# Feed-forward of a hybrid retention and attention layer: steps placed by product number, and other buffer counts

## Chip, cores and metric

The kernel runs on one core of one Trainium2 chip. Time is device microseconds of one execution. The kernel before was run three times: 3031.91, 3032.76 and 3039.37 us, median 3032.76. A separate execution was profiled; all rows of the profile are of that one.

## The reference, cut to what matters

One layer over 2048 positions of width 1024, with 256 positions of context. After a norm and a modulation, one projection gives the inputs of a retention in both directions (4 heads) and of an attention over context and sequence (8 heads). Their outputs go through `w_out` and are added to x. Then comes the part that the change rewrites:

```python
h2 = _modulate(_rmsnorm(x, norm2_g), sh2, sc2)
x = x + g2 * _sqrelu_mlp(h2, w_ff1, w_ff2)      # square(relu(h @ w1)) @ w2, 4096 wide
return _rmsnorm(x, final_norm_g)
```

## The kernel before

**Stages.** The first 690 us make the projections. From there to 1644 us the attention runs in numbered steps, with the retention and the output projection placed between its steps. The feed-forward fills the rest: *up products* (`h @ w1`) to 2358, then *down products* (`@ w2`) to 3008.

**Arithmetic.** Each f32 operand is split in an f16 `hi` and an f16 remainder `lo` (ACT copies `hi`, another engine subtracts it to get `lo`), and three f16 matmuls (hi·hi, hi·lo, lo·hi) stand for one. On top of that, blocks of 2 by 2 are multiplied with seven products in place of eight: sums of the operands' blocks are formed first, and sums of the seven products give the four results. So a *product* here is 4 x 3 = 12 matmuls of 128 x 512 in one PSUM bank, and each weight or activation block has four sums and seven *forms* (a form is a `hi` and `lo` pair).

**Up.** The 2048 positions are two halves (`hs[0]`, `hs[1]`) whose seven h forms lie in SBUF. w1 is taken in 16 blocks of 256 columns. `ITEMS` lists the work: the first `AHEAD` = 6 blocks for half 0 alone, ten blocks for both halves, and the first six again for half 1, since half 1's h forms are made later. 22 items, 32 block-halves, 224 products. For each item, `fetch_w1` (L1470) loads two tiles of w1, `sum_w1` (L1477, POOL) makes four sums, `form_w1` makes seven forms (L1487 ACT, L1488 DVE), and `up_part` (L1503 to L1505) does the matmuls. `up_out` takes a product out of PSUM: product 0 by an ACT copy (L1525), the others by DVE adds (L1515). A finished block gets its relu (L1519, ACT) and square (L1520, POOL) and is stored in DRAM as `u` (L1544).

Two more jobs run beside this: `h_pair(1, j)` makes half 1's h forms (L1368 POOL sums, L70 and L71 forms), and `w2_steps` makes the forms of w2 (L1554 loads, L1559 POOL sums, L1563 and L1564 forms, L1570 stores to `wf`).

**Down.** Four rounds `rd`, each with four of the 16 w2 blocks, and in each eight pairs of position tiles: 32 pairs, 224 products. `fetch_w2` (L1670) loads a round's seven 1 MB weight forms, `fetch_u` (L1680) a pair's four `ur` blocks, `fetch_y` (L1690) its two rows of x. `prepare(p, i)` makes the sums (L1694 POOL) and the form i of pair p (L70, L71). `down` (L1715 to L1717) does the matmuls, `down_out` takes them out (L1733 ACT copy for product 0, L1728 DVE adds), and `gate` multiplies by g2 and adds to y (L1755, L1756, both POOL, but the last ones DVE). y is stored after each round. In round 3 the final norm follows: ACT squares (L1764), a DVE sum (L1776), two small POOL operations for the root (L1009, L1010), a DVE scaling (L1782), the store (L1785).

**Order.** Each engine works through its own queue in program order, and the program order is written by hand (`manual_schedule`). Attention steps are placed in a table by step number and phase (`on`, `run`). The feed-forward is not: `up_jobs` and `down_jobs` are loops that emit, for each product, its matmuls, then the next item's sum and form, then `up_out` or `down_out`, and then a few steps from lists (`rest`, `pairs`, `later`, `gates`, `written`). All of a form, or all of a gate with its square, is emitted in one go. SP issues nearly all DMAs, also in program order.

A buffer *ring* hands out slots of several pools in turn: `w` for forms (7, with 3 more late), `r` for results (6, with 5 more), PSUM banks (4, with 2 more). Pools of the side `xp` have tags with a count each: `xr` 3, `hb` 2, `hp` 2, `w1s` 4, `hu` 3, `u` 2.

Of the kernel before, what the change touches and what calls it, by code (L numbers as in the profile page):

```python
# [22 lines left out]
P = 128  # L23
# [17 lines left out]
POOL_PAIRS = (0, 2, 4, 6, 7)  # L41

# [12 lines left out]
def layer_kernel(ctx: ExitStack, tc: tile.TileContext, a: dict, out: bass.AP):  # L55
# [1154 lines left out]
    def output_weights(k0):  # L1210
# [3 lines left out]
        def gates(i):  # L1214
            g = w_["g", i] = xp.tile([P, D], F32, name="g1b", tag="hb", bufs=2)
            nc.sync.dma_start(g, g1_d[i].partition_broadcast(P))

        def fetch(k, n):
            w = xp.tile([P, 2, 512], F32, name="wos", tag="xr", bufs=3)
            src = a["w_out"][0, k * P : (k + 2) * P, n * 512 : (n + 1) * 512]  # L1220
            nc.sync.dma_start(w, src.rearrange("(k p) n -> p k n", p=P))
            w_[k, n], w_[k + 1, n] = w[:, 0], w[:, 1]
# [25 lines left out]
    def output_tile(t, k, last):  # L1248
        y = {}

        def fetch_x():
            y["x"] = xp.tile([P, D], F32, name="xr", tag="xr", bufs=3)
            nc.sync.dma_start(y["x"], a["x"][0, t * P : (t + 1) * P, :])
# [103 lines left out]
    def h_pair(hf, j):  # L1357
# [3 lines left out]
        def fetch(g):  # L1361
            w = xp.tile([P, KT, P], F32, name="hb", tag="hb", bufs=2)
# [7 lines left out]
        def form(i, w):  # L1370
            if hf == 1:
                f = hs[1, i][:, :, :, j * P : (j + 1) * P]
                split16(f[:, 0], f[:, 1], x[w], nc.gpsimd if i % 2 else nc.vector)
                return
            f = xp.tile([P, 2, 4, P], F16, name="hp", tag="hp", bufs=2)
# [16 lines left out]
        return [lambda at=at: step(*at) for at in steps] + [store] * (hf == 0)  # L1392
# [18 lines left out]
    AHEAD = 6  # L1411
# [3 lines left out]
    ff = {"job": 0}  # L1415
# [3 lines left out]
    class Ring:  # L1419
# [7 lines left out]
        def extend(self, pool, tag, n):  # L1427
            self.slots += [(pool, tag, n)] * n
# [9 lines left out]
    def open_early():  # L1438
# [3 lines left out]
        ff["w"] = Ring((pool(early_ff, "fw"), "w", 7))  # L1442
        ff["r"] = Ring((pool(early_ff, "fr"), "r", 6))
# [19 lines left out]
    def fetch_w1(n):  # L1463
# [3 lines left out]
        for i in range(2):  # L1467
            w = xp.tile([P, D], F32, name="w1r", tag="xr", bufs=3).rearrange("p (k n) -> p k n", k=4)
# [5 lines left out]
    def sum_w1(n, to, x, y, op):  # L1474
        if n < len(ITEMS):
            s = raw1[n, to] = xp.tile([P, 4, P], F32, name="w1s", tag="w1s", bufs=4)
            nc.gpsimd.tensor_tensor(s, raw1[n, x], raw1[n, y], op=op)  # L1477

# [4 lines left out]
    def form_w1(n, i):  # L1483
        if n < len(ITEMS):
            w = w1[n, i] = ff["w"].tile([P, 2, 4, P], F16, "w1f")
            src = raw1.pop((n, FORMS1[i])) if i > 2 else raw1[n, FORMS1[i]]
            nc.scalar.activation(w[:, 0], src, AF.Copy, scale=sc1)  # L1487
            nc.vector.scalar_tensor_tensor(w[:, 1], src, sc1, w[:, 0], op0=ALU.mult, op1=ALU.subtract)  # L1488

# [5 lines left out]
    stores = []  # L1495
# [11 lines left out]
    def up_out(n, i, hf):  # L1507
# [10 lines left out]
        def done(r, f, tg):  # L1518
            nc.scalar.activation(r, r, AF.Relu, scale=scu)  # L1519
            nc.gpsimd.tensor_tensor(r, r, r, op=ALU.mult)  # L1520
            stores.append((ff["job"], ITEMS[n][0], hf, 2 * tg + f, r))
# [18 lines left out]
    def store_u():  # L1540
        _, b, hf, blk, r = stores.pop(0)
# [4 lines left out]
    def w2_steps(b):  # L1546


        x = {}
        rd, slot = PLACE[b]  # L1550

        def fetch(f):
            w = xp.tile([P, D], F32, name="w2r", tag="hb", bufs=2)
            nc.sync.dma_start(w, a["w_ff2"][0, b * FB + f * P : b * FB + (f + 1) * P, :])  # L1554
            x[f"b{f + 1}1"], x[f"b{f + 1}2"] = w[:, :512], w[:, 512:]

        def add(to, p, q, at=None):
            x[to] = x[at] if at else xp.tile([P, 512], F32, name="w2s", tag="hu", bufs=3)
            nc.gpsimd.tensor_tensor(x[to], x[p], x[q], op=ALU.subtract)  # L1559

        def form(i, w):
            f = xp.tile([P, 2, 512], F16, name="w2f", tag="hp", bufs=2)
            nc.scalar.activation(f[:, 0], x[w], AF.Copy, scale=scw)  # L1563
            nc.vector.scalar_tensor_tensor(f[:, 1], x[w], scw, f[:, 0], op0=ALU.mult, op1=ALU.subtract)  # L1564
            x["made"] = i, f

        def store():
            if "made" in x:
                i, f = x.pop("made")
                nc.sync.dma_start(wf_d[rd][i][:, slot], f)  # L1570

        steps = [(add, "t1", "b12", "b11"), (form, 0, "b11"), (add, "t2", "b22", "t1")]
        steps += [(form, 5, "t1"), (add, "t3", "b22", "b12", "b12"), (form, 2, "t2"), (add, "t4", "b21", "t2", "t1")]
        steps += [(form, 1, "b21"), (form, 3, "t3"), (form, 6, "b22"), (form, 4, "t4")]

        def step(fn, *at):
            store()
            fn(*at)

        return [lambda f=f: fetch(f) for f in range(2)] + [lambda at=at: step(*at) for at in steps] + [store]  # L1580

    def prelude(k0):
# [3 lines left out]
        on(k0 - 2, "late", sum_w1, 0, *SUMS1[0])  # L1586
        on(k0 - 1, "late", sum_w1, 0, *SUMS1[1])
        on(k0, "begin", open_early)
        for i in range(7):
            on(k0 + i // 2, "dma", fetch_h, i)  # L1590
            on(k0 + 2 + 2 * i, "late", form_w1, 0, i)
        on(k0, "late", sum_w1, 0, *SUMS1[2])
        on(k0 + 3, "late", sum_w1, 0, *SUMS1[3])
        on(k0 + 16, "dma", fetch_w1, 1)
        for i in range(4):
            for k in range(4):
                on(k0 + 14 + 4 * i + k, "pe", up_part, 0, i, 0, k)
            on(k0 + 17 + 4 * i, "late", up_out, 0, i, 0)
# [292 lines left out]
```

## Time and profile before

| what | value |
|---|---|
| median of three runs | 3032.76 us |
| profiled execution | 3028.91 us, its span 3027.1 us |
| mean granted TensorE clock | 0.972 |
| busy in the span | PE 2731.4, DVE 2045.8, POOL 1933.3, ACT 1409.7 us |
| up products, first to last start | 1644.5 to 2357.9 us (2688 matmuls) |
| down products, first to last start | 2358.2 to 3007.8 us (2688 matmuls) |

PE is TensorE, DVE VectorE, ACT ScalarE, POOL GpSimd, SP the engine that issues DMAs. `L1503` is a line of the kernel. A name left of `<-` is written, right of it read. In a wait row, "A <- B: t, n, m" means that engine A's instruction waited for B's, t us in total, n times, m at the longest. In a row of a single instruction the first number is its start, the second its duration, and the bracket the idle time of its engine ahead of it with what ended it. Rows "min/median/max" are in ns. A busy time of PE says little of its rate, as matmuls overlap; the count of matmuls in a stretch says more.

### The profile page before, as it was taken

The numbers are of one execution on the slowest core, as the hardware profiler recorded it, in microseconds if no ns is written. First come the engines' busy times: TensorE is split into PE (matmuls) and PEld (weight loads), VectorE is DVE, ScalarE is ACT, GpSimd is POOL, SyncE is SP. The second block draws the span as 40 slices with busy tenths as digits, with TensorE's granted clock in tenths as the row PEclk, the third lists the DMA queues.
The fourth block names the chain that finished last, engine by engine and source line by source line (L and its number), as shares of the span: only waits on it lengthen the run. The fifth ranks groups of instructions, "written<-read, shape, count | busy, mean of one in ns | idle before, by whom it ended". The sixth has DMA issues, their size and how long they took to land. (4 is left out here: it accounts for less than half of the span.)

```text
span 3027.1 us, 45947 instructions
## 1 busy us (share of the span) xinstructions
PE 2731.4 (90%) x16756; PEld 1614.5 (53%) x16756; DVE 2045.8 (68%) x3086; ACT 1409.7 (47%) x2349; POOL 1933.3 (64%) x1549
## 2 busy tenths in 40 slices
PE   7998899998799999899998978898988799999985
PEld 4777677776566665566665433343333344444432
DVE  5889747448987777787774456666665466666555
ACT  3333334326777777777776334444443222222222
POOL 2536336237856668875666566565564599999865
PEclk9999999999999999999999999999999899999988
DMA  9988743527211213441124434555574657575432
GB/s 298 335 290 283 256 143 94 171 87 224 79 55 61 82 55 101 115 120 48 59 76 167 139 106 150 183 182 184 171 249 134 223 179 265 176 265 176 147 125 98
DMA packets 330657, 480.71 MB, mean 159 GB/s; under 512 B 82999, under 2 KB 195895, under 8 KB 325950
## 3 DMA queue, kind: packets, MB, share of 16 engines
q1 hardware_dynamic: 320150, 470.28, 47.9%
q10 hardware_dynamic: 10280, 7.48, 0.8%
q8 instruction: 132, 2.16, 0.3%
q14 instruction: 95, 0.78, 0.1%
HBM read 325.47 MB, written 152.20 MB: 158 GB/s over the span
## 5 line engine op out<-in xcount | busy, mean ns | idle before, releaser
L180 DVE TENSOR_REDUCE nm<-mp 128x1 f32<-128x512 f32 (+1 forms) x576 | 391.0, 685 | 168.3 <-PE mp L167 139.9
L221 POOL TENSOR_TENSOR plo<-p,phi 128x1024 f16<-128x1024 f32 x160 | 353.8, 2212 | 172.1 <-ACT phi L214 142.4
L210 ACT ACTIVATE p<-st 128x512 f32<-128x512 f32 x576 | 338.3, 597 | 186.5 <-PE st L205 116.0
L1503 PE MATMUL pu<-hf,w1f 128*128 128x512 f16 x896 | 347.9, 388 | 73.3 <-DVE r L1515 68.0
L1715 PE MATMUL pd<-w,uf 128*128 128x512 f16 x896 | 345.9, 386 | 51.8 <-ACT d L1733 44.5
L1504 PE MATMUL pu<-hf,w1f 128*128 128x512 f16 x896 | 347.6, 388 | 1.3 <-POOL hf L71 1.1
L1505 PE MATMUL pu<-hf,w1f 128*128 128x512 f16 x896 | 347.5, 388 | 0.0
L1716 PE MATMUL pd<-w,uf 128*128 128x512 f16 x896 | 345.7, 386 | 0.0
L1717 PE MATMUL pd<-w,uf 128*128 128x512 f16 x896 | 345.5, 386 | 0.0
L824 PE MATMUL pso<-whi,hi_l 128*128 128x512 f32 (+1 forms) x768 | 294.7, 386 | 10.5 <-ACT xs L526 4.7
L214 ACT ACTIVATE phi<-p 128x1024 f16<-128x1024 f32 x288 | 303.9, 1055 | 0.0
L1520 POOL TENSOR_TENSOR r<-r 128x512 f32<-128x512 f32 x128 | 137.6, 1076 | 248.2 <-ACT r L1519 243.6
L826 PE MATMUL pso<-whi,lo_l 128*128 128x512 f32 (+1 forms) x768 | 292.2, 381 | 3.8 <-DVE lo_l L67 3.8
L825 PE MATMUL pso<-wlo,hi_l 128*128 128x512 f32 (+1 forms) x768 | 292.2, 381 | 1.2 <-DVE wlo L67 1.1
L237 PE MATMUL o<-wv,plo 128*128 128x65 f16 x2304 | 234.5, 193 | 24.0 <-POOL plo L221 16.7
L223 DVE TENSOR_TENSOR plo<-p,phi 128x512 f16<-128x512 f32 x256 | 240.1, 939 | 18.4 <-ACT phi L214 15.8
L71 DVE TENSOR_TENSOR uf<-ur,uf 128x512 f16<-128x512 f32 x128 | 143.3, 1130 | 160.7 <-ACT uf L70 160.6
L238 PE MATMUL o<-wv,phi 128*128 128x129 f16 x2304 | 242.4, 220 | 0.0
L237 PEld LDWEIGHTS <-plo 128*128 128x128 f16 x2304 | 205.9, 98 | 58.8 <-POOL plo L221 26.2
L204 PE MATMUL st<-qr,ks 128*128 128x512 f16 x576 | 219.5, 381 | 15.0 <-ACT p L210 14.8
L205 PE MATMUL st<-qr,ks 128*128 128x512 f16 x576 | 219.4, 381 | 0.1
L167 PE MATMUL mp<-ks,qr 128*128 128x512 f16 x512 | 196.1, 383 | 23.5 <-DVE nm L180 23.4
(326 smaller groups left out, 6142.2 us busy)
## 6 DMA issues: line engine op xcount, KB each, us to landing
wm<-in_w_ff SPq DMA_DIRECT2D x64, 512.0 KB, 5.5
u<-r SPq DMA_DIRECT2D x128, 256.0 KB, 3.0
ur<-u SPq DMA_DIRECT2D x128, 256.0 KB, 5.1
y<-x SPq DMA_DIRECT2D x64, 512.0 KB, 6.5
wst<-in_w_in SPq DMA_DIRECT2D x60, 512.0 KB, 5.9
wf<-w2f SPq DMA_DIRECT2D x112, 256.0 KB, 2.2
w<-wf SPq DMA_DIRECT2D x28, 1024.0 KB, 12.5
x<-y SPq DMA_DIRECT2D x48, 512.0 KB, 3.6
```

The lines of the kernel that those rows point to most:

```text
L180: nc.vector.tensor_reduce(dst, src, axis=AX.X, op=ALU.max, negate=True)
L210: nc.scalar.activation(self.p[kt // 2][:, kt % 2], self.s.pop(kt), AF.Exp, scale=HD**-0.5)
L214: nc.scalar.activation(hi, self.p[j], AF.Copy)
L221: nc.gpsimd.tensor_tensor(lo, p, hi, op=ALU.subtract)
L237: mm(o[:, : HD + 1], lo[:, i, c], v[:, : HD + 1], start=False, stop=False)
L824: mm(ps[:, :width], hi[:, k], wh, start=k == 0, stop=False)
L1503: mm(pu[hf, i], whi, hi, start=k == 0, stop=False)
L1504: mm(pu[hf, i], whi, lo, start=False, stop=False)
L1505: mm(pu[hf, i], wlo, hi, start=False, stop=k == 3)
L1715: mm(ps, u[:, 0, b], w[:, b, 0], start=b == 0, stop=False)
L1716: mm(ps, u[:, 0, b], w[:, b, 1], start=False, stop=False)
L1717: mm(ps, u[:, 1, b], w[:, b, 0], start=False, stop=b == 3)
```

## The change

The loops of `up_jobs` and `down_jobs` go. Each piece of work becomes an entry of the table `on(step, phase, ...)`, where the step is the number of a product (`NU` is the number of up products that are left after the first four, and the down products count on from there). In each step the phases run in one order: matmuls, POOL sums, `hi`, `lo`, relu, out, square, late, DMA. A form's `lo` stands one step behind its `hi`, a relu one step behind the add, a square two, a store four; loads stand 2 to 11 steps ahead. `AHEAD` goes from 6 to 8, so the items are 8, 8 and 8. `h_pair` loses its branch for half 1, and `h_forms` and `w2_forms` share a new function `seven`. In `gate` the add to y goes to DVE for the second 512 columns. Buffer counts change (`xr` 4, `hb` 4, `hp` 4, `w1s` 6; the early rings `w` 6 and `r` 4), the PSUM ring gets two more banks once the last attention tile is done, and the scratch space for dynamic DMA is set to 1024.

```diff
+XR, HB, HP, W1S = 4, 4, 4, 6
...
-    AHEAD = 6
+    AHEAD = 8
...
         def extend(self, pool, tag, n):
-            self.slots += [(pool, tag, n)] * n
+            at = self.n % max(len(self.slots), 1)
+            self.slots = [(pool, tag, n)] * n + self.slots[at:] + self.slots[:at]
...
-        ff["w"] = Ring((pool(early_ff, "fw"), "w", 7))
-        ff["r"] = Ring((pool(early_ff, "fr"), "r", 6))
+        ff["w"] = Ring((pool(early_ff, "fw"), "w", 6))
+        ff["r"] = Ring((pool(early_ff, "fr"), "r", 4))
...
+    def hi_w1(n, i):
...
+            nc.scalar.activation(w[:, 0], raw1[n, FORMS1[i]], AF.Copy, scale=sc1)
+    def lo_w1(n, i):
...
             nc.vector.scalar_tensor_tensor(w[:, 1], src, sc1, w[:, 0], op0=ALU.mult, op1=ALU.subtract)
...
-    def up_out(n, i, hf):
+    def up_out(at, n, i, hf):
...
         def done(r, f, tg):
-            nc.scalar.activation(r, r, AF.Relu, scale=scu)
-            nc.gpsimd.tensor_tensor(r, r, r, op=ALU.mult)
-            stores.append((ff["job"], ITEMS[n][0], hf, 2 * tg + f, r))
+            on(at + 1, "relu", lambda: nc.scalar.activation(r, r, AF.Relu, scale=scu))
+            on(at + 2, "square", lambda: nc.gpsimd.tensor_tensor(r, r, r, op=ALU.mult))
+            on(at + 4, "dma", store_u, ITEMS[n][0], hf, 2 * tg + f, r)
...
+    def seven(b0, source, tiles, low, kinds, scale=None):
...
+        for g in range(2):
+            on(b0 - 5 + g, "dma", fetch, g)
+        sums = [("t1", "b12", "b11"), ("t2", "b22", "t1"), ("t3", "b22", "b12", "b12"), ("t4", "b21", "t2", "t1")]
+        for at, s in zip((0, 1, 2, 4), sums):
+            on(b0 + at, "sum", add, *s)
+        for at, w in enumerate(("b11", "b21", "t1", "t2", "b22", "t3", "t4")):
+            on(b0 + at, "hi", hi, w)
+            on(b0 + at + 1, "lo", lo, w)
+            if low[1]:
+                on(b0 + at + 3, "dma", lambda w=w: low[1](kinds[w], x["f", w]))
...
-        on(k0 + 16, "dma", fetch_w1, 1)
+        on(k0 + 10, "dma", fetch_w1, 1)
...
+    JOBS = [(n, i, hf) for n, (_, hfs) in enumerate(ITEMS) for i in range(7) for hf in hfs][4:]
+    NU = len(JOBS)
     def up_jobs():
...
+        for j, (n, i, hf) in enumerate(JOBS):
+            first.setdefault((n, i), j)
+            for k in range(4):
+                on(j, "pe", up_part, n, i, hf, k)
+            on(j, "out", up_out, j, n, i, hf)
+        for n in range(len(ITEMS) - 1):
+            for i in range(7):
+                if (n, i) in first:
+                    at = first[n, i] + len(ITEMS[n][1]) - 1
+                    on(at, "hi", hi_w1, n + 1, i)
+                    on(at + 1, "lo", lo_w1, n + 1, i)
+            on(first.get((n, 0), 0), "dma", fetch_w1, n + 2)
+            if n > 0:
+                for i in range(2):
+                    on(first[n - 1, 5 + i], "sum", sum_w1, n + 1, i)
+                    on(first[n, i], "sum", sum_w1, n + 1, 2 + i)
+        on(0, "late", lambda: last3[0](0))
+        for j in range(4):
+            h_forms(5 + 10 * j, j)
+        first1 = first[AHEAD, 0]
+        for m, b in enumerate(PLACE):
+            w2_forms(first1 + 1 + 7 * m, b)
+        for i in range(7):
+            on(first[NB, 0] + 2 + 2 * i, "dma", fetch_w2, 0, i)
...
+    def gate(at, p, g, n, c):
...
+        on(at + 1, "square", lambda: eng.tensor_tensor(c, c, ff["g2"][:, s], op=ALU.mult))
+        eng2 = nc.vector if n or fast else nc.gpsimd
+        on(at + 2, "lo" if eng2 is nc.vector else "square", lambda: eng2.tensor_tensor(y, y, c, op=ALU.add))
+        if not final:
+            if n == 1:
+                on(at + 4, "dma", lambda: nc.sync.dma_start(x1_d[tiles_of(p)[g]], ys.pop((p, g))))
             return
...
+        on(at + 3, "relu", square)
         if n == 1:
+            on(at + 4, "lo", ending, at + 4, p, g)
...
     def down_jobs():
         for i in range(7):
-            fetch_w2(1, i)
+            on(NU + 1 + i // 2, "dma", fetch_w2, 1, i)
...
+            s = NU + 7 * p
+            for m, blk in enumerate((2, 3, 0, 1)):
+                on(s - 11 + m // 2, "dma", fetch_u, p, blk)
+            for g in range(2):
+                on(s - 3 + g, "dma", fetch_y, p, g)
+            on(s - 7, "sum", sum_u, p, "s1", "a21", "a22", ALU.add)
+            on(s - 6, "sum", sum_u, p, "s2", "s1", "a11", ALU.subtract)
+            on(s - 5, "sum", sum_u, p, "s3", "a11", "a21", ALU.subtract, "a21")
+            on(s - 3, "sum", sum_u, p, "s4", "a12", "s2", ALU.subtract, "s2")
             for i in range(7):
+                on(s - 7 + i, "hi", hi_u, p, i)
+                on(s - 6 + i, "lo", lo_u, p, i)
+                on(s + i, "pe", down, p, i)
+                on(s + i, "out", down_out, s + i, p, i)
                 if (hf, q) == (1, 3) and rd in (0, 1):
-                    fetch_w2(rd + 2, i)
+                    on(s + i + 1, "dma", fetch_w2, rd + 2, i)
+    FPHASES = ("pe", "sum", "hi", "lo", "relu", "out", "square", "late", "dma")
...
+        while events:
+            for phase in FPHASES:
+                run(k, phase)
+                if phase == "late" and rest:
+                    rest_steps(2)
+                    if not rest:
+                        banks.close()
+                        ff["ps"].extend(pool(late_ff, "fp3", space=PSUM), "p", 2)
+            k += 1
...
-    nc = bacc.Bacc("TRN2", target_bir_lowering=False, num_devices=1)
+    nc = bacc.Bacc("TRN2", target_bir_lowering=False, num_devices=1, dynamic_dma_scratch_size=1024)
```

296 lines of the change are left out of this document (113 added, 183 removed).

## The prediction, as it was made

> **What bounds the kernel now.** I read the page's busy times first, then a table of stretches, then the waits of each stretch, then single engines in order of time.
>
> ```profile
> span 3027.1 us, 45947 instructions
> 1644.50:1690.00 45.50, 33.62 (x139) 15.68 (x138) 15.48 (x24) 9.30 (x18) 13.68 (x14) 0.82 0.51 182
> 1690.00:1740.00 50.00, 50.00 (x233) 22.78 (x231) 27.94 (x36) 20.11 (x32) 33.00 (x26) 0.99 0.43 138
> 1740.00:1830.00 90.00, 67.13 (x267) 27.57 (x265) 50.84 (x58) 38.16 (x63) 61.41 (x48) 0.89 0.34 100
> 1830.00:1900.00 70.00, 67.53 (x310) 30.14 (x309) 45.62 (x55) 28.98 (x44) 41.35 (x32) 1.00 0.58 185
> 1900.00:2350.00 450.00, 400.67 (x1781) 175.90 (x1780) 280.26 (x337) 191.81 (x294) 251.52 (x191) 0.97 0.56 181
> 2350.00:2400.00 50.00, 28.84 (x123) 12.49 (x122) 17.54 (x22) 12.21 (x21) 18.39 (x15) 0.77 0.73 259
> 2400.00:2820.00 420.00, 420.00 (x1945) 190.32 (x1944) 273.00 (x327) 104.49 (x184) 410.99 (x279) 1.00 0.63 208
> 2820.00:3008.00 188.00, 157.40 (x662) 67.17 (x660) 99.52 (x131) 50.50 (x114) 132.88 (x118) 0.93 0.38 121
> 3008.00:3027.10 19.10, 0.17 (x1) 0.00 (x0) 12.10 (x18) 2.89 (x8) 6.86 (x10) 0.60 0.23 86
> ```
>
> After the stretch come its length, then busy time and instructions of PE, weight loads, DVE, ACT and POOL, then the granted clock, DMA share and GB/s. From 2400 to 2820 TensorE never rests and does 1945 matmuls in 420 us, 0.216 us each. A product of 12 matmuls so costs 2.59 us, and no order of the other engines can go below that. What a stretch loses is its length less its matmuls at 0.216:
>
> - 1644 to 1690, the last attention tile and the first products: 119 matmuls of 512 columns (25.7) and 20 transposes (about 2.6) leave **17 us**.
> - 1690 to 1740: nothing.
> - 1740 to 1830, while the second half's h forms are made: 90 - 57.7 = **32**.
> - 1830 to 2350: 3 + 65 = **68**.
> - 2350 to 2400, from the up products to the down products: 50 - 26.6 = **23**.
> - 2820 to 3008, round 3 of the down products: 188 - 143 = **45**.
> - the tail without products: **19**.
>
> That is 204 us lost in 1383. In the up stretch the losses have this cause:
>
> ```profile
> ACT r L1519 <- DVE r L1515: 237.6, 118, 7.3
> DVE w1f L1488 <- ACT w1f L1487: 139.7, 82, 5.5
> ACT w1f L1487 <- POOL w1s L1477: 81.8, 31, 4.8
> PE pu L1503 <- DVE r L1515: 68.0, 54, 7.6
> 2344.32 1.02 DVE L1488 SCALAR_TENSOR_TENSOR w1f<-w1r,sc,w1f 128x512 f16<-128x512 f32 x1 [1.40 <-ACT w1f L1487]
> 2345.26 0.68 DVE L1515 TENSOR_TENSOR r<-pu,r 128x512 f32<-128x512 f32 x1
> 2345.97 0.72 ACT L1519 ACTIVATE r<-r,scu 128x512 f32<-128x512 f32 x1 [1.69 <-DVE r L1515]
> 2346.60 0.71 ACT L1487 ACTIVATE w1f<-w1s,sc 128x512 f16<-128x512 f32 x1
> 2347.34 1.02 DVE L1488 SCALAR_TENSOR_TENSOR w1f<-w1s,sc,w1f 128x512 f16<-128x512 f32 x1 [1.40 <-ACT w1f L1487]
> ```
>
> The reader sees a ring. DVE adds a product out of PSUM, ACT takes its relu, behind it in ACT's queue stands the next `hi`, DVE's `lo` waits for that, and DVE's next add stands behind the `lo`. One turn, 2344.32 to 2347.34, is 3.02 us, more than the 2.59 of a product, and TensorE then waits for a PSUM bank (68.0 us). When POOL is late with a sum, the same ring stops whole (81.8 us).
>
> ```profile
> ACT uf L70 <- DMA ur<-u: 27.2, 3, 23.3
> PE pd L1715 <- ACT d L1733: 21.2, 1, 21.2
> 2371.12 3.70 SPq L1670 DMA_DIRECT2D w<-wf  x7
> 2374.88 23.47 SPq L1680 DMA_DIRECT2D ur<-u  x8
> ACT junk L1764 <- POOL y L1756: 126.2, 27, 6.2
> PE pd L1715 <- ACT d L1733: 23.3, 6, 4.2
> ```
>
> At the change of stage pair 1's `ur` loads are issued behind seven 1 MB weight loads; ACT's first form waits 23.3 us for them, with the copy of product 0 queued behind it. In round 3 ACT's square waits for POOL's gate of the same step (126.2), and again the copy out of PSUM stands behind it.
>
> **The change, part by part.**
>
> *The ring (1740 to 2350).* A form's `hi` now stands ahead of the relu in ACT's step, its `lo` a step later, the relu a step after its add. A turn of the ring spreads over two products, 5.18 us against 3.02 of work. What is late next is whichever of DVE and POOL has most to do. Their prices:
>
> ```profile
> L1515 DVE TENSOR_TENSOR r<-pu,r x224: 673/678/692, 1650.5 to 2368.1; 128x512 f32<-128x512 f32 x112
> L1488 DVE SCALAR_TENSOR_TENSOR w1f<-w1s,sc,w1f x88: 736/992/1795, 1641.4 to 2350.4; 128x512 f16<-128x512 f32 x88
> L71 DVE TENSOR_TENSOR uf<-ur,uf x128: 679/1152/1755, 2354.9 to 2994.7; 128x512 f16<-128x512 f32 x128
> L1782 DVE SCALAR_TENSOR_TENSOR y<-y,cy_e,fgb x18: 743/1279/2279, 2854.9 to 3023.3; 128x1024 f32<-128x1024 f32 x14, 128x512 f32<-128x512 f32 x4
> L1520 POOL TENSOR_TENSOR r<-r x128: 1037/1039/1572, 1673.3 to 2369.6; 128x512 f32<-128x512 f32 x128
> 2604.18 1.71 POOL L1756 TENSOR_TENSOR y<-y,d 128x512 f32<-128x512 f32 x1
> 2605.86 1.71 POOL L1755 TENSOR_TENSOR d<-d,g2b 128x512 f32<-128x512 f32 x1
> 2610.55 1.27 POOL L1694 TENSOR_TENSOR us<-us,ur 128x512 f32<-128x512 f32 x1
> 2611.77 1.27 POOL L1755 TENSOR_TENSOR d<-d,g2b 128x512 f32<-128x512 f32 x1
> L1010 POOL TENSOR_TENSOR cy_e<-cv_e,half 128x1 f32<-128x1 f32 x15 | 8.2, 549 | 1.2
> ```
>
> The PSUM add never varies (673 to 692 ns), but a DVE operation with both inputs in SBUF goes from 679 to 1755, and POOL's starts lie 1.22 us apart alone (2610.55 to 2611.77) and 1.68 beside one (2604.18 to 2605.86). So I price a POOL operation at 1.22, a square at 1.04, and each DVE operation with two SBUF inputs at 0.46 of POOL's time. Check on rounds 0 to 2: 12 x 1.22 + 7 x 0.46 = 17.9 us a pair, against 18.1 of products; POOL is 411 of 420 us busy there. It fits.
>
> Items with both halves, 14 products, 36.3 us: POOL has 12 sums (4 for w1, 8 for w2), 8 squares and 21 DVE operations beside them: 14.6 + 8.3 + 9.7 = 32.6. DVE has 21 at about 1.1 and 14 adds: 32.6. Both 90%: hidden. I leave 5 us of the 68, plus 2 for the r ring cut from 11 to 9 buffers: a copy or add can now wait a step for an `u` store, with DVE's or ACT's later steps behind it, and the eight PSUM banks (six before) cover some five products of that.
>
> The h forms (products 5 to 48): per 7 products, 18.1 us, POOL has 9.0 for the item, 0.7 x 7 x 1.22 = 6.0 for h, and 9.8 x 0.46 = 4.5: 19.5, 108%. Over 111 us POOL falls 9 us behind, some three products. Sums lead by two steps and the banks by five, and half 1's forms are first used in product 52; I leave 3 of the 32.
>
> AHEAD 6 to 8 adds two items: 14 `hi`, 14 `lo`, 8 sums, 4 loads of 512 KB, no matmul. They lie in items with one half, where POOL has 9.0 + 3.2 of 18.1; nothing. If that cover went, 14 x 1.1 + 8 x 1.22 = 25 us.
>
> *SP's queue.* Loads go 5 products (w1, w2) or 4 (`ur`) before use, stores 2 to 4 steps behind. A late square holds the store, and behind it SP's loads. At the change of stage `ur` of pair 1 is issued five steps ahead of the weights; pair 2's now stands behind those 7 MB. By ACT's wait these took until 2393.8, 22 us or 8 products from their issue, and pair 2 is first used 6 after it: POOL and ACT wait two or three products, which the banks cover. Of 23 I leave 2.
>
> *Round 3.* The square comes a step after the gate, and two of eight gate operations a pair go from POOL to DVE. POOL: 10 x 1.22 + 2 x 0.75 for the roots (0.55, and the small scaling before each, an estimate) = 13.7, nine DVE operations 4.1, two of twice the width 0.9 each: 19.6 against 18.1 us, 108%. Eight pairs make 12 us, which TensorE or the tail pays. Of 45 I leave 12. Rounds 0 to 2: 12.2 + 4.1 = 16.3, 90%; stays bound by TensorE.
>
> [...]
>
> *The first products.*
>
> ```profile
> ACT w1f L1487 <- DMA w1r<-in_w_ff: 5.7, 1, 5.7
> 1685.07 1.11 PE L1306 MATMUL bank<-ident,xr 128*128 128x128 f32 x4 [6.82 <-POOL xr L1301]
> ```
>
> Item 1's load goes six steps earlier, which takes most of the 5.7. The 6.82, the last tile's norm, stays: its transposes still stand behind product 4, and the slower clock after it. Of 17 I leave 12. The smaller DMA scratch I cost at nothing (all DMAs are issued by SP and ACT), and the deeper buffers before 1644 too: bounds 3 us either way, as TensorE is near full there.
>
> *Tail.*
>
> ```profile
> 3011.91 2.87 DVE L1728 TENSOR_TENSOR d<-pd,d 128x512 f32<-128x512 f32 x4
> ```
>
> DVE took the last products out of PSUM four us after TensorE's end at 3008; with less ahead of it, 15 of 19.
>
> **Sum.** Gains: 5 + 29 + 61 + 21 + 33 + 4 = 153. 3027.1 - 153 = 2874. The profiled execution took 3028.91, 1.8 above its span, and the median of the runs shown, 3032.76, lies 3.85 above that: **2880 us**. If the residuals are nothing but 12 at the start and 14 in the tail, 2854; if twice as large, about 2904.
>
> **Rivals.**
>
> 1. [...] Each DVE operation costs POOL its whole time alone (0.68, forms with scale 0.74, wide ones 1.28). Both halves: 22.9 + 15.5 = 38.4, 2.1 over, eight items: 17. h: 15 + 7.3 = 22.3, 4.2 over per 7, 26. Round 3: 13.7 + 6.1 + 2.6 = 22.4, 4.3 over, eight pairs: 34. 77 in place of 22: **2935**. Against it stands the check above. Chance 0.11.
> 2. *A transfer takes the ring's place.*
>
> ```profile
> ACT w2f L1563 <- DMA w2r<-in_w_ff: 35.2, 10, 6.3
> ACT w2f L1563 <- DMA wf<-w2f: 22.6, 20, 6.9
> ```
>
> These waits, 57.8 us, came when loads led by a step or two. If SP, held by late stores, loses the lead, most comes back: 2880 + 50 = **2930**. Against it: DMA share 0.56. Chance 0.09.
> 3. *It does not do what it says.* POOL stays more than a step late, so ACT waits at each `hi` and the ring closes again one step on: the 61 return, **2941**. For it: POOL at 90 to 108%. Chance 0.08.
> 4. *Slower.* The one engine that gets more everywhere is DVE. If every two-input operation took its longest (1.795, 1.755, 2.279): both halves 47.2 against 36.3, eight items 87; h 22.2 against 18.1, 25; rounds 0 to 2 with nine a pair 20.6 against 18.1, 24 pairs 59; round 3 25.1, 56. 227 in place of 22 turns the gain into a loss: **3085**. It decides from a mean of about 1.67 us. Against it: the medians 0.99 and 1.15. Chance 0.05.
>
> **How the numbers follow.** The forecast has 0.67, its own range 2850 to 2910 (2854 and 2904 with the bounds at the start). The range 2850 to 2935 takes in rivals 1 and 2 and leaves out 3 and 4. Faster by over 0.3% (about what a measurement of this kernel can tell from no change): 0.94; within: 0.01; slower: 0.05.
>
> **What would show it.** Right: about 233 matmuls per 50 us through the up products; ACT's wait for DVE's add no longer in TensorE's path; no stretch of 20 us without matmuls at the change of stage; round 3 at 19 to 20 us a pair with POOL over 95% busy. Wrong: waits of TensorE for DVE of over 20 us in the up stretch, DVE's `lo` at a mean over 1.4 us, ACT waiting for DMA, or a round 3 at 18.1.

## The result, and the profile after

The changed kernel takes **2863.45 us** (median of four runs, 2859.76 to 2864.69); the kernel before, run on the same chip, 3033.70. The ratio is 0.9434, 95% interval 0.9417 to 0.9450. The forecast was 2880, in a range of 2850 to 2935. The profiled execution took 2864.03 us.

First the page's span, then from the table of stretches (columns as before) the first products, all the rest of the feed-forward, three pieces of it and the tail:

```profile
span 2862.1 us, 46159 instructions
```

```profile
1647.80:1700.00 52.20, 39.63 (x167) 18.67 (x166) 19.99 (x31) 12.62 (x23) 20.42 (x21) 0.84 0.51 183
1700.00:2838.00 1138.00, 1136.70 (x5266) 514.85 (x5265) 943.70 (x1025) 462.53 (x754) 938.24 (x640) 1.00 0.62 206
1740.00:1830.00 90.00, 90.00 (x419) 40.83 (x417) 78.80 (x82) 47.18 (x76) 88.77 (x62) 1.00 0.54 164
2259.80:2300.00 40.20, 40.20 (x188) 18.24 (x187) 29.75 (x33) 10.90 (x20) 32.47 (x23) 1.00 0.83 313
2700.00:2750.00 50.00, 50.00 (x234) 22.65 (x232) 45.81 (x48) 18.21 (x39) 43.52 (x33) 1.00 0.52 179
2840.00:2862.10 22.10, 2.36 (x11) 0.88 (x9) 16.56 (x23) 4.33 (x12) 10.39 (x13) 0.62 0.25 95
```

The second stretch is the whole story: 5266 matmuls at 0.216 us are 1137.5 us of 1138. TensorE loses half a microsecond from 1700 to 2838, where the kernel before lost 168 (32 at the h forms, 68 in the rest of the up products, 23 at the change of stage, 45 in round 3). The loss that is left lies at the two ends. The first products hold 147 matmuls of 512 (31.75) and 20 transposes (2.6) in 52.2 us: 17.9 lost, against 17.2 by the same sum before. The last matmul starts at 2841.98; with 0.216 us for it the tail is 19.9, against 19.1 by the same sum before.

The waits from 1700 to 2260, the up products (total, times, longest, in us), and TensorE's own from 1640 to the end:

```profile
ACT r L1525 <- DVE r L1521: 145.5, 108, 4.6
POOL r L1526 <- ACT r L1525: 93.5, 41, 8.9
DVE r L1521 <- PE pu L1511: 85.1, 91, 2.2
ACT w2f L1568 <- DMA wf<-w2f: 39.5, 37, 3.7
```

```profile
PE bank L1307 <- POOL xr L1302: 10.7, 2, 6.8
PE pd L1728 <- DVE uf L1719: 1.2, 2, 0.6
PE bank L1260 <- DVE rl L1267: 1.2, 1, 1.2
```

ACT still waits 145.5 us for DVE's add, but nothing that TensorE needs stands behind it. The third row is the new sign: DVE now waits for TensorE's product, 91 times. Before, TensorE waited for DVE (68.0 us), and that wait is gone.

### The profile page after: what moved, and what is told of

Read it like the earlier page. It is cut to its first block, busy times and chain, and to the rows that moved or that the text cites. A ratio compares the mean times of both kernels' runs of the same rounds, so it can differ in the third digit from the quotient of the medians.

```text
span 2862.1 us, 46159 instructions
## 1 busy us (share of the span) xinstructions
PE 2689.7 (94%) x16756; PEld 1610.7 (56%) x16756; DVE 2205.3 (77%) x3162; ACT 1431.8 (50%) x2363; POOL 1932.5 (68%) x1495
## 4 chain that ended last, share of the span: by engine, by line
PE 55%; DVE 8%; POOL 5%; issue 3%; DMA 2%; ACT 1%; SPq 0%; POOLq 0%; DVEq 0%; ACTq 0%
PE pu L1509 7%; PE pu L1510 7%; PE pu L1511 7%; PE pd L1726 5%; PE pd L1727 5%; PE pd L1728 5%; PE o L239 3%; PE st L205 3%; PE st L206 3%; PE mp L168 2%; DVE nm L181 2%; DVE plo L224 2%; PE bank L1275 2%; PE bank L1277 2%; PE bank L1276 2%
## 5 line engine op out<-in xcount | busy, mean ns | idle before, releaser
L1509 PE MATMUL pu<-hf,w1f 128*128 128x512 f16 x896 | 340.9, 380 | 0.0
L1510 PE MATMUL pu<-hf,w1f 128*128 128x512 f16 x896 | 340.9, 380 | 0.0
L1728 PE MATMUL pd<-w,uf 128*128 128x512 f16 x896 | 339.6, 379 | 1.3 <-DVE uf L1719 1.2
L1511 PE MATMUL pu<-hf,w1f 128*128 128x512 f16 x896 | 340.7, 380 | 0.0
L1726 PE MATMUL pd<-w,uf 128*128 128x512 f16 x896 | 339.6, 379 | 0.0
L1727 PE MATMUL pd<-w,uf 128*128 128x512 f16 x896 | 339.6, 379 | 0.0
L238 PE MATMUL o<-wv,plo 128*128 128x65 f16 x2304 | 234.9, 193 | 26.2 <-POOL plo L222 18.1
L224 DVE TENSOR_TENSOR plo<-p,phi 128x512 f16<-128x512 f32 x256 | 243.3, 951 | 16.5 <-ACT phi L215 15.9
L1766 POOL TENSOR_TENSOR d<-d,g2b 128x512 f32<-128x512 f32 x126 | 200.5, 1592 | 70.1 <-DVE d L1738 68.3
L1521 DVE TENSOR_TENSOR r<-pu,r 128x512 f32<-128x512 f32 x224 | 150.9, 685 | 115.3 <-PE pu L1511 93.8
L1526 POOL TENSOR_TENSOR r<-r 128x512 f32<-128x512 f32 x128 | 168.4, 1320 | 94.0 <-ACT r L1525 93.5
```

The source lines that it names most:

```text
L238: mm(o[:, : HD + 1], lo[:, i, c], v[:, : HD + 1], start=False, stop=False)
L1509: mm(pu[hf, i], whi, hi, start=k == 0, stop=False)
L1510: mm(pu[hf, i], whi, lo, start=False, stop=False)
L1511: mm(pu[hf, i], wlo, hi, start=False, stop=k == 3)
L1726: mm(ps, u[:, 0, b], w[:, b, 0], start=b == 0, stop=False)
L1727: mm(ps, u[:, 0, b], w[:, b, 1], start=False, stop=False)
```

## The experiments

Two numbers are given for each run: the ratio to the kernel before on the same chip, and the time from the first up product's first matmul to the end of the span of its profiled execution. The second leaves out when the feed-forward begins, which moved between 1641.8 and 1650.9 us among kernels that have the changed kernel's code up to there.

| run | median us | ratio, 95% interval | first up product to end, us | against |
|---|---|---|---|---|
| before | 3033.70 | 1 | 1382.6 | |
| after | 2863.45 | 0.9434 (0.9417 to 0.9450) | 1214.0 | -168.6 to before |
| relu later, in the kernel before | 2953.26 | 0.9741 (0.9728 to 0.9755) | 1306.6 | -76.0 to before |
| ring closed | 2919.97 | 0.9626 (0.9613 to 0.9639) | 1271.4 | +57.4 to after |
| relu in its add's step | 2861.80 | 0.9435 (0.9423 to 0.9448) | 1212.9 | -1.1 |
| six banks | 2865.54 | 0.9442 (0.9428 to 0.9457) | 1211.9 | -2.1 |
| `ur` behind the weights | 2860.71 | 0.9437 (0.9424 to 0.9450) | 1212.4 | -1.6 |
| pair 1 late | 2874.41 | 0.9466 (0.9443 to 0.9488) | 1226.4 | +12.4 |
| gate adds on POOL | 2869.63 | 0.9467 (0.9454 to 0.9480) | 1222.6 | +8.6 |
| gate closed behind the copy | 2865.32 | 0.9460 (0.9444 to 0.9476) | 1220.1 | +6.1 |
| gates first | 2888.10 | 0.9515 (0.9493 to 0.9538) | 1239.2 | +25.2 |
| gates first, adds on POOL | 2889.45 | 0.9521 (0.9501 to 0.9541) | 1240.7 | +26.7 |
| first products mended | 2847.82 | 0.9397 (0.9384 to 0.9410) | 1199.5 | -14.5 |
| the same, ending later | 2844.96 | 0.9381 (0.9358 to 0.9405) | 1198.6 | -15.4 |

Theory: the order of the steps made the loss. Rival: room did (eight banks for six, more buffers).

**The ring, opened alone in the kernel before.** Relu and square of a finished block are kept back and issued a product later (the added call issues what is held). 128 of the 224 products finish a block.

```diff
         def done(r, f, tg):
-            nc.scalar.activation(r, r, AF.Relu, scale=scu)
-            nc.gpsimd.tensor_tensor(r, r, r, op=ALU.mult)
-            stores.append((ff["job"], ITEMS[n][0], hf, 2 * tg + f, r))
+            held.append((ITEMS[n][0], hf, 2 * tg + f, r))
...
+                    up_out(None, None, None)
                     up_out(n, i, hf)
```

> The kernel before with one thing changed: relu and square of an up product are issued one product later, behind the next `hi` and `lo` and ahead of the next add. Buffers, six banks, AHEAD 6, stores, change of stage and down products are those of before. Order theory: TensorE's 68 us of waits for DVE's add and a good part of the 81.8 of ACT for POOL go: 40 to 70 us faster than before, 2963 to 2993; the stretch of the h forms (32 lost) stays, since its own chain is untouched. Room theory: within 15 us of before, 3018 to 3034.

It came out 76 to 78 us faster, more than either theory had put. Three stretches, and TensorE's wait from 1640 to 2960:

```profile
1740.00:1830.00 90.00, 81.23 (x364) 35.62 (x363) 59.85 (x72) 42.54 (x70) 76.01 (x55) 0.98 0.43 128
1900.00:2250.00 350.00, 330.89 (x1517) 148.43 (x1516) 233.03 (x297) 167.32 (x260) 225.36 (x168) 0.99 0.67 217
2300.00:2350.00 50.00, 38.12 (x169) 16.75 (x167) 24.50 (x30) 10.65 (x19) 31.76 (x21) 0.86 0.67 249
```

```profile
PE pu L1503 <- DVE r L1515: 23.2, 16, 7.6
```

TensorE's wait for DVE's add falls from 68.0 to 23.2. The stretch of the h forms loses 90 - 364 x 0.216 = 11 in place of 32: it had the ring too, against the expectation. Moving the relu and the square back by a product gives nearly half of the whole change (76.0 of 168.6).

**The ring, closed in the changed kernel.** All its room stays; `same` is a phase right behind `out`.

```diff
-            on(at + 1, "relu", lambda: nc.scalar.activation(r, r, AF.Relu, scale=scu))
-            on(at + 2, "square", lambda: nc.gpsimd.tensor_tensor(r, r, r, op=ALU.mult))
+            on(at + (at == 0), "same", lambda: nc.scalar.activation(r, r, AF.Relu, scale=scu))
+            on(at + (at == 0), "square", lambda: nc.gpsimd.tensor_tensor(r, r, r, op=ALU.mult))
...
-                    on(at + 1, "lo", lo_w1, n + 1, i)
+                    on(at, "lo", lo_w1, n + 1, i)
...
-            on(b0 + at + 1, "lo", lo, w)
+            on(b0 + at, "lo", lo, w)
```

> The changed kernel with its up products closed again: each `lo` in its `hi`'s step, relu and square in their add's step; eight PSUM banks, deeper buffers and AHEAD 8 stay. Order theory (the ring add, relu, hi, lo, add in one step set the pace): a turn of 3.02 us against 2.59 a product comes back, 2863 + 60 to 100 = 2925 to 2965, and DVE's wait for PE before the PSUM add falls. Room theory (banks and buffers did it): within 10 us of the changed kernel, 2863 to 2873.

57 us slower; the expectation was 60 to 100, and 10 by the rival, which falls. TensorE's wait and the busy times of two stretches, then one turn of the ring in order of time (start, duration, engine, line):

```profile
PE pu L1509 <- DVE r L1521: 38.4, 36, 1.6
```

```profile
2000.00:2050.00 50.00, 42.81 (x194) 18.76 (x193) 37.70 (x42) 23.21 (x36) 33.26 (x25) 1.00 0.67 211
2250.00:2300.00 50.00, 50.00 (x234) 22.62 (x233) 34.85 (x42) 23.19 (x37) 32.63 (x24) 1.00 0.43 119
```

```profile
2054.38 0.68 DVE L1521 TENSOR_TENSOR r<-pu,r 128x512 f32<-128x512 f32 x1
2055.09 0.72 ACT L1525 ACTIVATE r<-r,scu 128x512 f32<-128x512 f32 x1 [1.69 <-DVE r L1521]
2055.72 0.71 ACT L1485 ACTIVATE w1f<-w1s,sc 128x512 f16<-128x512 f32 x1
2056.33 0.71 ACT L1568 ACTIVATE w2f<-b,scw 128x512 f16<-128x512 f32 x1
2056.45 0.91 DVE L1491 SCALAR_TENSOR_TENSOR w1f<-w1s,sc,w1f 128x512 f16<-128x512 f32 x1 [1.40 <-ACT w1f L1485]
2057.29 1.52 DVE L1574 SCALAR_TENSOR_TENSOR w2f<-b,scw,w2f 128x512 f16<-128x512 f32 x1
2058.73 0.68 DVE L1521 TENSOR_TENSOR r<-pu,r 128x512 f32<-128x512 f32 x1
```

From add to add is 4.35 us in a step with two forms. On the average of 2000 to 2050 a product takes 50 x 12 / 194 = 3.09 us, with DVE, the busiest engine beside TensorE, 75% busy. Closing the ring brings back 57 of the 100 us that the up products lost before. The rest goes with what stayed in this kernel (sums and loads issued further ahead, buffers, `AHEAD` 8), and no run takes that apart.

From 2250 to 2300, with one form a step, the closed ring loses nothing. A turn with a relu takes 3.02 us there too, but only four of seven products have a relu:

```profile
2263.36 0.72 ACT L1525 ACTIVATE r<-r,scu 128x512 f32<-128x512 f32 x1 [2.75 <-DVE r L1521]
2266.38 0.72 ACT L1525 ACTIVATE r<-r,scu 128x512 f32<-128x512 f32 x1 [1.69 <-DVE r L1521]
```

The first relu of the next seven products starts at 2280.05, so the ring does seven in 16.7 us, under TensorE's 18.1. In the kernel before, the last items with one form a step took 19.3 us each (such relus start at 2323.69 and 2342.95), and between them ACT waited for a sum of POOL:

```profile
2337.64 0.72 ACT L1487 ACTIVATE w1f<-w1s,sc 128x512 f16<-128x512 f32 x1 [3.07 <-POOL w1s L1477]
```

So the closed ring costs time where a second form stands in the step, or a sum comes late; the turn of 3.02 us alone does not.

**Which of the two lags.** Only the relu goes back into its add's step; `lo` stays a step behind `hi`.

```diff
-            on(at + 1, "relu", lambda: nc.scalar.activation(r, r, AF.Relu, scale=scu))
+            on(at + (at == 0), "same", lambda: nc.scalar.activation(r, r, AF.Relu, scale=scu))
```

> Only the relu is put back into its add's step, right behind it; `lo` stays a step behind `hi`. Order theory: the turn add, relu, hi, lo, add still spans two products (3.0 us in 5.2), so 0 to 5 us, 2863 to 2868. If every lag is needed by itself: most of the 60 to 100 of the closed ring, over 2900. Room theory: 0.

No difference: a ratio of 0.9435 against 0.9434. The lag of `lo` alone keeps the ring open. The lag of the relu alone, with `hi` and `lo` in one step, was run only in the kernel before.

**Six banks.**

```diff
-                        ff["ps"].extend(pool(late_ff, "fp3", space=PSUM), "p", 2)
```

> The changed kernel with six PSUM banks for the feed-forward products, as the kernel before had (the two banks of the attention are not handed over). Order theory: the banks only cover short lateness; 0 to 6 us, 2863 to 2869, most of it while the h forms are made and at the change of stage. Room theory: the waits of TensorE for a bank come back, 20 us or more, over 2883.

No difference either (0.9442). With the steps in this order, the cover that the prediction leaned on isn't drawn. The buffer counts of before, `AHEAD` 6 and the larger DMA scratch were not tried in the changed order.

**Change of stage, two steps.** First `ur` of pair 1 behind the weights, all issued at the last up product; then all of it four products later, sums and forms too, as the kernel before had it behind the last stores of u.

```diff
-            on(NU + 1 + i // 2, "dma", fetch_w2, 1, i)
+            on(NU - 1, "dma", fetch_w2, 1, i)
...
-                on(s - 11 + m // 2, "dma", fetch_u, p, blk)
+                on(NU - 1 if p == 1 else s - 11 + m // 2, "dma", fetch_u, p, blk)
```

In the second, NU + 3 stands for both NU - 1, and

```diff
+            d = 4 if p == 1 else 0
...
-            on(s - 7, "sum", sum_u, p, "s1", "a21", "a22", ALU.add)
+            on(s - 7 + d, "sum", sum_u, p, "s1", "a21", "a22", ALU.add)
...
-                on(s - 7 + i, "hi", hi_u, p, i)
+                on(s - 7 + d + i, "hi", hi_u, p, i)
```

> The changed kernel with one piece of order undone: pair 1's four `ur` loads are issued right behind the seven 1 MB weight loads of round 1, at the last up product. Order theory: ACT's first form of pair 1 waits some 27 us for them (3.7 + 23.5 in the kernel before), with the copy of pair 0's product 0 behind it; eight banks and pair 0's own forms cover seven products, 18 us, so 10 to 20 us slower, 2873 to 2883, with a wait of ACT for `ur` of over 20 us. Room theory (eight banks cover it whole): within 4 us, 2859 to 2867.

> The changed kernel with pair 1 as late as before: its weights of round 1, and behind them its four `ur` loads, are issued at the fourth down product, behind the last stores of u, and its sums and forms move four products with them. Issued about 10 us after the last up product, the ur land some 25 us later; with sums and forms behind them, 4 us, that is 39 us, and pair 0's seven products cover 18: 15 to 25 us slower, 2878 to 2888, one wait of TensorE for pair 1's forms. If the place of these loads did not matter: within 4 us, 2859 to 2867.

The first: no difference, where the theory had 10 to 20. ACT's wait is there, but 13.4 us long. The second: 12.4 us slower (10 by the ratio), under the 15 to 25. In the first kernel and then the second, the waits around the change of stage, and a stretch of the second:

```profile
POOL us L1711 <- DMA ur<-u: 14.3, 1, 14.3
ACT uf L1715 <- DMA ur<-u: 13.4, 1, 13.4
```

```profile
ACT uf L1715 <- DMA ur<-u: 21.2, 2, 21.0
PE pd L1726 <- ACT uf L1715: 6.8, 1, 6.8
PE pd L1728 <- DVE uf L1719: 4.0, 3, 2.3
```

```profile
2280.00:2290.00 10.00, 3.48 (x10) 1.27 (x11) 3.50 (x4) 1.89 (x3) 4.71 (x4) 0.66 1.03 380
```

Pair 0's seven products are 18 us of work for TensorE. A wait of 13.4 us fits under them, one of 21.0 with sums and forms behind it doesn't. So what counts here is the hour at which the transfers are issued, not which of them stands first. The kernel before lost 23 here; 11 of these are not brought back by this edit, and their cause stays open.

**Round 3.** Four kernels undo its parts. In the first, all gate adds are on POOL again.

```diff
-        eng2 = nc.vector if n or fast else nc.gpsimd
+        eng2 = nc.vector if fast else nc.gpsimd
```

In the second the gate is closed up: scaling, add and square one step behind the product, still behind that step's copy or add out of PSUM.

```diff
-        on(at + 2, "lo" if eng2 is nc.vector else "square", lambda: eng2.tensor_tensor(y, y, c, op=ALU.add))
+        on(at + 1, "square", lambda: eng2.tensor_tensor(y, y, c, op=ALU.add))
...
-        on(at + 3, "relu", square)
+        on(at + 1, "late", square)
```

In the third all three stand in a phase ahead of `out`, as before, and each `lo` in its `hi`'s step; the fourth is the third with the first one's edit.

```diff
-FPHASES = ("pe", "sum", "hi", "lo", "relu", "out", "square", "late", "dma")
+FPHASES = ("pe", "sum", "hi", "lo", "relu", "gate", "out", "square", "late", "dma")
...
-        on(at + 3, "relu", square)
+        on(at + 1, "gate", square)
...
-                on(s - 6 + i, "lo", lo_u, p, i)
+                on(s - 7 + i, "lo", lo_u, p, i)
```

> The changed kernel with all gate adds of the down products on POOL again (but in the last pair). By the price formula of the prediction a moved add costs POOL 1.22 - 0.46 = 0.76: rounds 0 to 2 17.9 us a pair, hidden under 18.1; round 3 21.1, so 12 us more than the changed kernel: 2875. By what the changed kernel's round 3 shows (POOL 44 of 50 us busy, 16.0 a pair) it comes to 17.5 and stays hidden: 0 to 5 us, 2863 to 2868. If the move was what freed round 3, 20 us or more: over 2883.

> The changed kernel with round 3's gate closed up: scaling, add and ACT's square of a half tile all a step behind the product, instead of one, two and three steps; the adds stay shared between DVE and POOL. Order theory: ACT's square waits for the add of its own step, with the next `hi` and the copy out of PSUM behind it, and DVE's add waits for POOL's scaling with its next PSUM add behind it: 15 to 45 us slower, 2878 to 2908, all of it in round 3, some in rounds 0 to 2. If the load of POOL alone decided: within 5 us, 2858 to 2868.

> The changed kernel with the down products' order of before in three points: a half tile's scaling, add and square are issued in the next step ahead of its copy or add out of PSUM, and each `lo` in its `hi`'s step. The adds stay shared between DVE and POOL, eight banks stay. Order theory in its full form (what matters is what stands ahead of the copy out of PSUM): ACT's copy of product 0 and DVE's adds wait for the gate, 15 to 45 us slower, 2878 to 2908. If eight banks and the lighter POOL are enough by themselves: within 6 us, 2857 to 2869.

> As the run with the gates first, and all gate adds on POOL too, so that of the change to round 3 only the eight banks and the deeper buffers are left. If order and POOL's load work together: most of the 45 us that round 3 lost before, 2893 to 2915, more than the 7 us of moving the adds alone and the 2 of closing the gate alone. If the banks were what freed round 3: under 15 us, up to 2878.

Moving the adds back costs 6 to 10 us by the three readings (median, ratio, profile), between the two estimates. Closing the gate behind the copy costs 2 to 8: near the 5 that were allowed if POOL's load alone decided, and under the order theory's 15 to 45. Putting it ahead of the copy, with each `lo` in its `hi`'s step, costs 25, within the order theory's 15 to 45. With the adds on POOL as well it costs hardly more, where 30 to 52 had been expected. The waits of round 3 (from 2650) with the gate closed behind the copy, then with gates first, and a stretch of the latter:

```profile
ACT junk L1778 <- POOL y L1768: 86.6, 16, 7.8
```

```profile
ACT junk L1778 <- POOL y L1768: 82.2, 14, 8.1
DVE uf L1719 <- ACT uf L1715: 50.2, 26, 3.2
```

```profile
2750.00:2800.00 50.00, 44.93 (x192) 17.82 (x190) 35.23 (x43) 14.93 (x34) 34.34 (x29) 0.97 0.37 126
```

About the same wait of ACT, 86.6 and 82.2 us (54.1 in the changed kernel), goes with 2 to 8 us in one kernel and 25 in the other. In the second the copy of product 0 and the next `hi` stand behind it, and DVE's `lo` waits 50.2 us. That kernel also has each `lo` in its `hi`'s step, and the two were not run apart. POOL is busy 34 of 50 us while TensorE does 192 matmuls, where the changed kernel does 233.

None of these costs is the whole effect on round 3, because forms are made ahead of TensorE and this lead hides a slower pace until it is used up. In the changed kernel, the `lo` of a pair's first form and the pair's first matmul, for the first and the last pair of round 3:

```profile
2681.06 1.75 DVE L1719 TENSOR_TENSOR uf<-ur,uf 128x512 f16<-128x512 f32 x1
2695.34 0.38 PE L1726 MATMUL pd<-w,uf 128*128 128x512 f16 x1
2820.38 1.76 DVE L1719 TENSOR_TENSOR uf<-ur,uf 128x512 f16<-128x512 f32 x1
2822.25 0.38 PE L1726 MATMUL pd<-w,uf 128*128 128x512 f16 x1
```

The lead falls from 12.5 us to 0.1. TensorE takes 18.1 us a pair to the end; the forms come every 18.1 us at first and every 20.7 us for the last four pairs. The same count in the other kernels, from their traces:

| run | forms, us a pair at the end of round 3 | lead at its first pair, us | TensorE, us for its last three steps from pair to pair |
|---|---|---|---|
| after | 20.7 | 12.5 | 18.1, 18.1, 18.1 |
| gate adds on POOL | 22.4 | 13.9 | 18.1, 21.0, 22.4 |
| gate closed behind the copy | 21.8 | 10.9 | 18.1, 21.0, 21.8 |
| gates first | 24.4 | 14.7 | 25.9, 24.6, 24.2 |
| gates first, adds on POOL | 24.4 | 15.9 | 26.0, 24.2, 24.1 |

Each edit slows the forms, and TensorE pays from the pair at which the lead is gone. What sets the 20.7 us was not tested: from 2700 to 2750 POOL is 87% and DVE 92% busy, so neither is full. The kernel before lost 45 here, with 25 to 27 us a pair on TensorE in its last five steps, so 20 of them stay open: the eight banks, the earlier sums and the place of the endings were not separated.

**The first products, and the tail.** The norm of the last two tiles gets a tile of its own, the hf loads are spread, and the two gain rows are loaded later.

```diff
-            nc.gpsimd.tensor_scalar(y["x"], y["x"], y["r"], 1.0, op0=ALU.mult, op1=ALU.mult)
+            to = y["x"]
+            if t < 2:
+                to = xp.tile([P, D], F32, name="xn", tag="hb", bufs=HB)
+            nc.gpsimd.tensor_scalar(to, y["x"], y["r"], 1.0, op0=ALU.mult, op1=ALU.mult)
+            y["x"] = to
...
-            on(k0 + i // 2, "dma", fetch_h, i)
+            on(k0 + (0, 2, 4, 8, 12, 16, 20)[i], "dma", fetch_h, i)
...
+        on(60, "dma", lambda: nc.sync.dma_start(ff["g2"], gs_d.partition_broadcast(P)))
```

A second kernel has in addition, for the tail:

```diff
-            on(at + 4, "lo", ending, at + 4, p, g)
+            late = 4 if p == len(PAIRS) - 2 else 0
+            on(at + 4 + late, "lo", ending, at + 4 + late, p, g)
```

> The changed kernel with the first products mended: the norm of the last two tiles writes a tile of its own (it no longer waits for the store of x that reads its source), the seven 1 MB hf loads are spread over 21 steps in place of 4, and the loads of the two gain rows of the down stage go 60 products later. Theory (transfers: the w1r load and the x store stand behind the hf loads, and the norm behind the store): ACT's 4.6, POOL's 7.9 and 5.5 go, TensorE's 3.8 and most of its 6.8, and some of the slower clock behind them: 8 to 14 us faster than the changed kernel, 2849 to 2855. Rival (the last tile's own chain, products to adds, squares, root, norm, transposes, sets it): 0 to 4 us, 2859 to 2863.

> The kernel with the first products mended, and in the last but one pair the ending (sum of squares, root, output) four products later, so that DVE takes the last pair's products out of PSUM ahead of it. Theory: DVE's last adds, some seven us behind TensorE's end, come four to six us earlier, and the tail of 19.9 falls to 14 to 18: 2 to 6 us faster than the kernel with the first products mended, 2842 to 2846. Rival (DVE's own work, 14.4 of these 20 us, sets the tail in whatever order): within 2 us, 2846 to 2850.

The first is 14.5 us faster than the changed kernel (11 by the ratio). Its first products:

```profile
1650.50:1700.00 49.50, 45.64 (x222) 21.86 (x221) 28.61 (x40) 18.30 (x33) 28.46 (x24) 1.00 0.57 201
```

What held them in the changed kernel: a row of the waits from 1647.8 to 1700, single instructions of ACT and TensorE, and the stretch behind the longest wait.

```profile
POOL xr L1302 <- DMA x<-xr: 13.3, 2, 7.9
```

```profile
1658.07 0.72 ACT L1485 ACTIVATE w1f<-w1r,sc 128x512 f16<-128x512 f32 x1 [4.61 <-DMA w1r<-in_w_ff]
1689.22 1.11 PE L1307 MATMUL bank<-ident,xr 128*128 128x128 f32 x4 [6.84 <-POOL xr L1302]
1690.13 0.63 PE L1509 MATMUL pu<-hf,w1f 128*128 128x512 f16 x1
1690.56 0.63 PE L1510 MATMUL pu<-hf,w1f 128*128 128x512 f16 x1
```

```profile
1689.00:1692.00 3.00, 2.78 (x9) 1.60 (x10) 1.57 (x2) 0.00 (x0) 1.29 (x2) 0.50 0.66 239
```

The norm overwrites the tile that the store of x still reads, so POOL waits for a transfer (13.3 us in two waits), which in SP's queue stands behind the 7 MB of hf loads, or behind the gain rows, and TensorE waits for POOL. Then it starts again at a granted clock of 0.50, with matmuls 0.43 us apart, until 1695.2. With the waits gone the clock stays at 1.00 and 222 - 20 matmuls (43.6) and the transposes (2.6) leave 3.3 lost of 17.9. The three edits were not run apart.

The second is the fastest kernel of the study, 2844.96 us. What the later ending adds is 0.9 us by the profile, 2.9 by the medians and 4.9 by the ratios, so these runs don't decide between the theory's 2 to 6 and the rival's 2. DVE is done with the last products 4.5 us after TensorE's end in place of 9.4, and then has the ending still before it. Its own work fills most of the tail, 13.8 of the last 19.8 us:

```profile
2824.19 4.26 DVE L1742 TENSOR_TENSOR d<-pd,d 128x512 f32<-128x512 f32 x6
```

```profile
2824.00:2843.80 19.80, 0.86 (x4) 0.20 (x2) 13.83 (x22) 4.10 (x12) 11.12 (x12) 0.61 0.28 106
```

## Why the prediction was right, and where its sizes were off

The mechanism held: a ring of DVE and ACT set the pace of the up products, and order opened it. By the prediction's terms, in us gained:

| term | forecast | measured |
|---|---|---|
| h forms | 29 | 32 |
| rest of the up products | 61 | 68 |
| change of stage | 21 | 23 |
| round 3 | 33 | 45 |
| first products | 5 | -0.7 |
| tail | 4 | -0.8 |
| stage before, bound 3 either way | 0 | -3.6 |

The measured terms make 163 where the spans differ by 165.0; the forecast's made 153. Four terms came out 24 us better than forecast and the last three 14 us worse, so it is in part luck that the total is only 10 off. The rest of the 16.6 us between forecast and result is the step from the span to the median: 5.65 was added, and it was 1.35 (2863.45 - 2862.1).

- **The ring.** Right, and shown from both sides: opened alone -76, closed +57. The residuals of 5, 3 and 2 us were not there. The h forms were priced at 108% of POOL; POOL was in fact 88.77 of 90 us busy, the w1 forms kept a lead of 11 to 14 us over their use, and TensorE never waited. The prediction took the turn of 3.02 us for the pace of the ring; that a turn this long comes only in four of seven products, that it took a second form or a late sum to cost time, and that the lag of `lo` alone is enough, it did not see.
- **Banks as cover.** The prediction let banks cover lateness at the h forms; six were enough there, too. At the change of stage pair 0's own products did the covering.
- **Round 3: the slower pace came, but TensorE did not pay for it.** The term was 19.6 us a pair for POOL, so 12 us over eight pairs, "which TensorE or the tail pays". The forms did slow down, to 20.7 us a pair. The step that failed is who pays: the forms' lead of 12.5 us over TensorE took it all, 2.6 us a pair, and the sum had given this lead no credit. So TensorE stayed at 18.1 us a pair, which the prediction had named as a sign against itself. POOL was 87% busy (43.52 of 50 us, 18.0 in a pair of 20.7), not over 95%. That the lead lasted just to the last pair is luck: the four kernels of the table in which it ran out sooner lost 2 to 27 us.
- **Rival 1, each DVE operation costing POOL its whole time** (2935), did not come. It needed 22.3 us of POOL for seven products at the h forms and 22.4 a pair in round 3; POOL was busy 17.9 and 18.0. By its price, 12 x 1.22 + 7 x 0.68 = 19.4 us, rounds 0 to 2 of the kernel before would not have run in 18.1 a pair either. The run with the adds on POOL, 8.6 us worse, doesn't test it: by this rival, too, a moved add costs POOL less, 0.68 us in place of the 1.22 of doing it.
- **The transfer in the ring's place** (2930) and **the ring closing again** (2941) did not come: ACT's longest wait for `wf` was 3.7 us, and TensorE's waits for DVE came to 1.2 us. **Slower** (3085) needed a DVE mean of 1.67; the `lo` of w1 had 0.99 and 1.15 us. The gate adds on DVE did pass that mean, at 1.70, but there are only 64.
- **The first products.** The forecast's gain of 5 was to come from ACT's wait of 5.7 us for the load of w1. Counted from the first up product, the load was issued 7.9 us earlier but landed only 1.1 us earlier, as 7 MB of hf loads ahead of it kept the DMA engines full (share 1.02 from 1640 to 1650); ACT still waited 4.61. And without that wait the store of x would have been the next. "What is late next" was asked of each engine here, and not of the DMA queue. Behind the wait of 6.84 us TensorE ran at a granted clock of 0.50 until 1695.2, as it did in the kernel before behind the 6.82 (0.50 from 1685.07 to 1690); in the kernel whose waits there are at most 1.7 the clock was 1.00 over the whole stretch.
- **Tail.** 15 was forecast, 19.9 came. DVE was to have less ahead of it, but took the last add out of PSUM 9.4 us after TensorE's last matmul, where it had been 6.6: at the end of round 3 DVE runs behind TensorE. Issuing the ending later brought 0.9 to 4.9 us; the bulk is DVE's own work.
- **The start.** Its 3.6 us are within what executions of the same code vary (9 us).

## What to carry to other kernels

When TensorE waits and no other engine is full (DVE, the busiest, was 75% busy in the closed ring), look for a ring: follow one instruction from step to step, add up the durations over several steps, as a single long turn can be made good by short ones (3.02 us in four of seven products, 16.7 for the seven), and compare the sum with the bound. Here one step of lag gave 76 us, and taking two PSUM banks away again cost nothing that could be measured. A wait cost time only through what was queued behind it (ACT waited 145.5 us for DVE's add while TensorE lost half a microsecond), and a slower pace only once the lead of the prepared work was used up (in the changed kernel the forms came every 20.7 us against TensorE's 18.1, and a lead of 12.5 us took it); so ask how large that lead is and whether it lasts to the end. Where a step lies behind a transfer, ask at what hour the transfer is issued and what bytes stand ahead of it, and look for a write that has to wait until a store has read its tile (13.3 us of POOL here).

## What the runs showed of the hardware beyond that

From 1740 to 1830 POOL was 98.6% busy (88.77 of 90 us) beside a DVE at 88%, with no loss on TensorE. The price of running side by side fell on both. POOL's square has a mean of 1078 ns in the up products before and of 1320 after, in the busier mix. DVE's gate add has a mean of 1701 ns, and takes 0.69 us in the tail while POOL is idle (at 2852.81); the same add on POOL has a mean of 1454 and takes 1271 at its shortest in round 3.

```profile
L1526 POOL TENSOR_TENSOR r<-r 128x512 f32<-128x512 f32 x128 | 168.4, 1320 | 94.0 <-ACT r L1525 93.5
L1768 DVE TENSOR_TENSOR y<-y,d 128x512 f32<-128x512 f32 x64 | 108.8, 1701 | 7.1 <-POOL d L1766 7.0
L1768 POOL TENSOR_TENSOR y<-y,d 128x512 f32<-128x512 f32 x64 | 93.1, 1454 | 4.5
```
